# Who makes four of fourteen lower parts of the token operand at a change of phase: VectorE or GpSimd

## The chip, the cores and the metric

The kernel runs on one core of one Trainium2 chip. The metric is device time in microseconds, the median of several executions. The profile and the trace are of one more execution, taken by the hardware profiler, with times from the start of its span.

## What is computed

One inference step of a one-layer hybrid decoder: 1024 prompt tokens and 8 x 4 sample tokens (1056 in all), model width 2048, in float32. The two large products are the ones that matter here:

```
hn   = rmsnorm(x, g_norm)                    # 1056 x 2048
proj = hn @ w_in                             # 2048 -> 5904 columns, cut into groups A to D
...                                          # A: gated convolution, B: gated linear attention,
                                             # C: sliding-window attention, D: attention to memory
mix  = concat(y_a, y_b, y_c, y_d)            # 1056 x 2048
y    = x + mix @ w_out                       # 2048 -> 2048
```

The states and caches of the groups are outputs too.

## The kernel before

**Layout.** The 1056 tokens lie along the free dimension, in two halves of 528 (`H`), and 128 features or columns on the partitions. A float32 operand is written as the sum of two rounded parts: an upper part made by a cast on ScalarE, and a lower part, the operand less its upper part, made by VectorE. A product is then three matmuls: upper by upper, lower weights by upper tokens, upper weights by lower tokens (L668).

**Seven products.** Column tiles are taken in pairs, and a pair's product over a 2 x 2 arrangement (two halves of the features by two column tiles, two halves of the tokens) is made with seven products in place of eight, in the order B11, T2, B21, T1, T3, B22, T4. Each of the seven needs one combination of the token operand, called a strand, and one of the weights. A strand of one phase covers 4 feature tiles of 128, that is 128 x 2112 values, and stays in SBUF as an upper and a lower tile (`self.S[i]`, from the pool `sp` with 14 buffers) for all pairs of the phase. The weights' combinations are made anew for each product (`make_weights`, cast at L644, lower part at L645, sums at L626 to L640), two products ahead.

**Four phases.** The features are worked off in two halves for `w_in` and two for `w_out`: phases one to four. `first_pair` makes a pair's seven products in the first half of a product's features and its result is written to DRAM (`keep`); `second_pair` loads it back as a base (L736, L745), ScalarE copies it into PSUM (L751), and the seven products are added onto it. Results leave PSUM through ScalarE copies (L701 to L718, L757, L764) and VectorE additions (L698, L761 to L778).

**The change of phase.** The strands of phase one are split by `first_strands`. For the three others they were written to DRAM by `combine` (`self.xs`), and the generator `strands` loads and splits them: 7 strands in two halves of 128 x 1056 each, 14 parts, at about 590, 1186 and 1383 us. It is advanced once after each product (`after`). From the last pair of the old phase on, it takes two new buffers for strand `i` (those which the old strand `i` gives back), and splits two halves: a cast at L429 on ScalarE and a subtraction at L430 on VectorE each. After each half the next load is issued (L563, queue SP) into a buffer of the pool `rt`, 10 buffers of 128 x 1056, which bases, results and other tiles use as well. So a load waits until the subtraction of an earlier part has given its buffer back. The first loads, `depth` of them (3, 2 and 6 at the three changes), are issued ahead. The parts are counted from 0 here: part `2*i + j` is half `j` of strand `i`.

**Order.** Each engine works off its own queue in order. The source gives the order in which work is asked for; the layer under it decides, when the program is built, in which order each engine's queue gets it and puts the waits in. In the trace the first subtraction at L430 (593.7 us) stands ahead of an addition at L698 that the source asks for earlier. PSUM has two tiles for the projections (`pj`), so a product can't begin before an earlier one's result has been read out, and in `second_pair` not before its base has been copied in. GpSimd is used for masks, a few clearings and seven subtractions of 128 x 512 at the start (L366).

```
        for c in range(2):
            for kk in range(4):
                ...
                for n, (w, x) in enumerate(((wh, sh), (wl, sh), (wh, sl))):
                    nc.tensor.matmul(ps[:, 512 * c : 512 * c + CG], w[:, ks], x[:, xs],
```

Of the kernel before, what the change touches and what calls it, by code (L numbers as in the profile page):

```python
# [7 lines left out]
F32 = mybir.dt.float32  # L8
# [3 lines left out]
ALU = mybir.AluOpType  # L12
# [110 lines left out]
class _Step:  # L123
# [291 lines left out]
                nc.vector.tensor_tensor(dst[:, cs], ps[i][c][:, 0:CW], self.R[:, cs], op=ALU.mult)  # L415


    def split(self, i, src, half=None):


        nc = self.nc
        if half is None:
            self.S[i] = self.stile(), self.stile()
        h, l = self.S[i]
        src = src if isinstance(src, list) else [src]
        w = 4 * H // len(src) if half is None else 2 * H
        for n, x in enumerate(src):
            s = slice((half or n) * w, (half or n) * w + w)
            nc.scalar.copy(h[:, s], x)  # L429
            nc.vector.tensor_tensor(l[:, s], x, h[:, s].bitcast(F32), op=ALU.subtract)  # L430

    def first_strands(self):

# [121 lines left out]
    def strands(self, ph, depth):  # L555

        parts = []

        def load():
            i, j = divmod(len(parts), 2)  # L560
            if i < 7:
                t = self.rtile("sx")
                self.nc.sync.dma_start(  # L563
                    out=t.rearrange("p (k t) -> p k t", k=2),
                    in_=self.xs[ph][2 * j : 2 * j + 2, :, PLACE[i], :].rearrange("k p t -> p k t"))
                parts.append(t)
        for _ in range(depth):
            load()
        while not self.turn:
            yield  # L570
        for i in range(7):
            yield
            self.S[i] = self.stile(), self.stile()
            for j in range(2):
                self.split(i, parts[2 * i + j], j)
                load()
        yield

# [1361 lines left out]
```

## Time and profile before

| | us |
|---|---|
| median of 3 runs | 1571.45 (1569.26 to 1574.41) |
| the profiled execution | 1575.27 |
| its span in the trace | 1573.5 |
| TensorE busy, matmuls | 1530.4 (97%) |
| VectorE busy | 1105.2 (70%) |
| ScalarE busy | 772.6 (49%) |
| GpSimd busy | 23.3 (1%) |
| mean granted TensorE clock | 0.985 |
| subtractions at L430 in the three changes (42) | 51.6 |

In the trace PE is TensorE, PEld its weight loads, DVE VectorE, ACT ScalarE, POOL GpSimd, and SP the queue that issues the transfers. A row of the timeline gives the start, the duration, the engine, the line, the operation, output and inputs with their shapes, a count, and in brackets how long the engine sat idle ahead of it and what released it. In a row of stretches each engine has its busy time and number of instructions, then come the granted clock (1.00 is full), the share of the DMA engines and the rate in GB/s. A row of waits gives the total, the number and the longest.

### The profile page before, as it was taken

The numbers are of one execution on the slowest core, as the hardware profiler recorded it, in microseconds if no ns is written. First come the engines' busy times: TensorE is split into PE (matmuls) and PEld (weight loads), VectorE is DVE, ScalarE is ACT, GpSimd is POOL, SyncE is SP. The second block draws the span as 40 slices with busy tenths as digits, with TensorE's granted clock in tenths as the row PEclk, the third lists the DMA queues.
The fourth block names the chain that finished last, engine by engine and source line by source line (L and its number), as shares of the span: only waits on it lengthen the run. The fifth ranks groups of instructions, "written<-read, shape, count | busy, mean of one in ns | idle before, by whom it ended". The sixth has DMA issues, their size and how long they took to land.

```text
span 1573.5 us, 30753 instructions
## 1 busy us (share of the span) xinstructions
PE 1530.4 (97%) x12194; PEld 1459.6 (93%) x12194; DVE 1105.2 (70%) x2283; ACT 772.6 (49%) x1620; POOL 23.3 (1%) x35
## 2 busy tenths in 40 slices
PE   7889999999999999999999999999998999999998
PEld 7668999999999999988998999999988999999998
DVE  8998645586555559665767776967779777596664
ACT  8466633322333336744468774645557443363332
POOL 3000000000000000000000000000000000000000
PEclk9899999999999999999999999999999999999999
DMA  7523222375332248158423333533437224587651
GB/s 272 193 92 109 69 103 94 142 267 193 109 110 100 95 148 308 62 144 298 139 78 84 109 90 121 173 123 90 167 119 244 82 104 168 188 288 267 209 203 63
DMA packets 102418, 236.77 MB, mean 150 GB/s; under 512 B 16516, under 2 KB 22532, under 8 KB 102276
## 3 DMA queue, kind: packets, MB, share of 16 engines
q1 hardware_dynamic: 102276, 234.82, 44.4%
q8 instruction: 96, 1.57, 0.4%
q14 instruction: 46, 0.38, 0.1%
HBM read 165.38 MB, written 69.41 MB: 149 GB/s over the span
## 4 chain that ended last, share of the span: by engine, by line
PE 75%; DVE 13%; ACT 5%; DMA 4%; issue 3%; SPq 0%; DVEq 0%; ACTq 0%
PE pj L668 64%; PE ms L902 2%; DVE wl L645 2%; DMA sx<-xs 1%; DVE s L430 1%; DVE xhl L311 1%; ACT wh L644 1%; ACT t L1280 1%; PE ms L1037 1%; DMA x<-in_xT 1%; ACT xhl L310 1%; DMA kc<-in_cache_mem_kT 1%; DVE t L1267 1%; PE ms L1313 1%; PE ms L1007 1%
## 5 line engine op out<-in xcount | busy, mean ns | idle before, releaser
L668 PE MATMUL pj<-s,wh 128*128 128x264 f32 x6720 | 1268.7, 288 | 7.6 <-ACT pj L751 5.5
L668 PEld LDWEIGHTS pj<-s,wh 128*128 128x128 f32 x6720 | 1055.5, 189 | 25.6 <-issue 12.7
L668 PE MATMUL pj<-s,wl 128*128 128x264 f32 x3360 | 960.3, 286 | 0.8 <-DVE wl L645 0.8
L668 PEld LDWEIGHTS pj<-s,wl 128*128 128x128 f32 x3360 | 636.7, 190 | 5.9 <-issue 4.1
L644 ACT CAST wh<-wr 128x512 fp32r<-128x512 f32 x300 | 186.3, 621 | 262.4 <-PE pj L668 248.3
L645 DVE TENSOR_TENSOR wl<-wr,wh 128x512 fp32r<-128x512 f32 x300 | 206.5, 688 | 119.8 <-ACT wh L644 119.4
L698 DVE TENSOR_TENSOR d<-d,pj 128x528 f32<-128x528 f32 x180 | 121.4, 701 | 102.1 <-PE pj L668 60.0
L644 ACT CAST wh<-ws 128x512 fp32r<-128x512 f32 x120 | 74.5, 621 | 93.9 <-PE pj L668 89.5
L645 DVE TENSOR_TENSOR wl<-ws,wh 128x512 fp32r<-128x512 f32 x120 | 82.5, 688 | 9.1 <-ACT wh L644 8.5
L751 ACT COPY pj<-d 128x528 f32<-128x528 f32 x120 | 72.5, 604 | 15.1 <-DVE u L761 5.5
L430 DVE TENSOR_TENSOR s<-sx,s 128x1056 fp32r<-128x1056 f32 x42 | 51.6, 1250 | 1.9 <-ACT s L429 1.9
L429 ACT CAST s<-sx 128x1056 fp32r<-128x1056 f32 x42 | 44.3, 1075 | 10.0 <-DMA sx<-xs 5.2
L772 DVE TENSOR_TENSOR d<-d,pj 128x528 f32<-128x528 f32 x30 | 21.1, 703 | 36.5 <-PE pj L668 36.5
L701 ACT COPY d<-pj 128x528 f32<-128x528 f32 x30 | 18.0, 599 | 55.1 <-PE pj L668 55.1
L707 ACT COPY d<-pj 128x528 f32<-128x528 f32 x30 | 18.0, 601 | 53.4 <-PE pj L668 53.4
L1280 ACT ACTIVATE t<-t,sm,sm 128x256 f32<-128x256 f32 (+1 forms) x64 | 37.1, 581 | 14.2 <-DVE sm L1272 14.2
L640 DVE TENSOR_TENSOR wr<-wr,ws 128x512 f32<-128x512 f32 x60 | 41.8, 697 | 1.0
L775 DVE TENSOR_TENSOR d<-u,pj 128x528 f32<-128x528 f32 x30 | 21.1, 703 | 30.1 <-PE pj L668 30.0
L626 DVE TENSOR_TENSOR ws<-wr,wr 128x512 f32<-128x512 f32 x60 | 41.3, 688 | 1.2
L636 DVE TENSOR_TENSOR wr<-wr,wr 128x512 f32<-128x512 f32 x60 | 41.3, 688 | 1.1
L627 DVE TENSOR_TENSOR ws<-ws,wr 128x512 f32<-128x512 f32 x60 | 41.3, 688 | 1.0
L778 DVE TENSOR_TENSOR d<-u,pj 128x528 f32<-128x528 f32 x30 | 21.1, 703 | 29.8 <-PE pj L668 29.6
(368 smaller groups left out, 1524.2 us busy)
## 6 DMA issues: line engine op xcount, KB each, us to landing
wr<-in_w_in SPq DMA_DIRECT2D x184, 256.0 KB
half_in<-d SPq DMA_DIRECT2D x44, 528.0 KB
d<-half_in SPq DMA_DIRECT2D x44, 528.0 KB
sx<-xs SPq DMA_DIRECT2D x42, 528.0 KB
wr<-in_w_out SPq DMA_DIRECT2D x64, 256.0 KB
x<-in_xT SPq DMA_DIRECT2D x24, 528.0 KB
xs<-t SPq DMA_DIRECT2D x36, 264.0 KB
half_out<-d SPq DMA_DIRECT2D x16, 528.0 KB
```

What stands on the lines that cost most here:

```text
L429: nc.scalar.copy(h[:, s], x)
L430: nc.vector.tensor_tensor(l[:, s], x, h[:, s].bitcast(F32), op=ALU.subtract)
L626: v.tensor_tensor(s1, r(1, 0), r(1, 1), op=ALU.add)
L627: v.tensor_tensor(s2, s1, r(0, 0), op=ALU.subtract)
L636: v.tensor_tensor(x, r(0, 0), x, op=ALU.subtract)
L640: v.tensor_tensor(x, x, self.wsum[n][1], op=ALU.subtract)
L644: nc.scalar.copy(wh, x)
L645: v.tensor_tensor(wl, x, wh.bitcast(F32), op=ALU.subtract)
L668: nc.tensor.matmul(ps[:, 512 * c : 512 * c + CG], w[:, ks], x[:, xs], start=(first and kk == 0 and n == 0), stop=(kk == 3 and n == 2), ski ...
L698: nc.vector.tensor_tensor(o, o, bank(ps), op=op)
L751: nc.scalar.copy(bank(ps), x)
L1280: nc.scalar.activation(ps[u][:, g, kts[0] : 2], ps[u][:, g, kts[0] : 2], AF.Exp, bias=mx[:, c : c + 1], scale=rq[:, 4 * m + c : 4 * m + c ...
```

## The change

`split` gets an argument for the engine of the subtraction. `strands` passes GpSimd for the second half (`j` is 1) of the strands with even `i` (0, 2, 4 and 6), that is for parts 1, 5, 9 and 13 of the fourteen, at each of the three changes. The other ten parts, all casts, all loads and `first_strands` stay as they were.

```diff
-    def split(self, i, src, half=None):
+    def split(self, i, src, half=None, eng=None):
...
             nc.scalar.copy(h[:, s], x)
-            nc.vector.tensor_tensor(l[:, s], x, h[:, s].bitcast(F32), op=ALU.subtract)
+            eng = eng or nc.vector
+            eng.tensor_tensor(l[:, s], x, h[:, s].bitcast(F32), op=ALU.subtract)
...
             for j in range(2):
-                self.split(i, parts[2 * i + j], j)
+
+                self.split(i, parts[2 * i + j], j, self.nc.gpsimd if j and i % 2 == 0 else None)
                 load()
```

## The prediction

> **What bounds the kernel now.** I read the page first. Its first part says what is full and its fifth which instructions the change touches.
>
> ```profile
> span 1573.5 us, 30753 instructions
> PE 1530.4 (97%) x12194; PEld 1459.6 (93%) x12194; DVE 1105.2 (70%) x2283; ACT 772.6 (49%) x1620; POOL 23.3 (1%) x35
> L645 DVE TENSOR_TENSOR wl<-wr,wh 128x512 fp32r<-128x512 f32 x300 | 206.5, 688 | 119.8 <-ACT wh L644 119.4
> L430 DVE TENSOR_TENSOR s<-sx,s 128x1056 fp32r<-128x1056 f32 x42 | 51.6, 1250 | 1.9 <-ACT s L429 1.9
> ```
>
> TensorE sets the end: 97% of the span, and with the rows below nearly all of the rest is in gaps that a few places make. GpSimd is almost unused, VectorE is at 70% on average. An average does not decide: the 42 subtractions at L430 lie in three short stretches, the changes of phase (14 each). So I looked at those next, each cut into the pair of products before the change and the pair after it (for the second change the stretch in which its 14 parts are made).
>
> ```profile
> core 0: us, PE busy (x) PEld busy (x) DVE busy (x) ACT busy (x) POOL busy (x), PEclk, DMA share, GB/s
> 589.70:611.30 21.60, 20.36 (x168) 20.14 (x166) 21.37 (x26) 17.98 (x24) 0.00 (x0) 1.00 0.94 331
> 611.30:631.50 20.20, 18.99 (x152) 18.70 (x153) 16.07 (x23) 9.23 (x15) 0.00 (x0) 1.00 0.75 260
> 1186.20:1220.50 34.30, 30.23 (x216) 28.32 (x215) 30.68 (x48) 23.59 (x37) 0.00 (x0) 0.90 0.71 230
> 1383.30:1403.10 19.80, 17.64 (x146) 17.43 (x145) 19.77 (x24) 17.25 (x23) 0.00 (x0) 1.00 0.99 333
> ```
>
> Here VectorE is the full engine (21.37 of 21.60, 19.77 of 19.80), the DMA engines are nearly as full (0.94 and 0.99 of their time), GpSimd does nothing, and TensorE loses a little. What it loses stands in its own timeline as idle time ahead of an instruction:
>
> ```profile
> 611.31 0.39 PE L668 MATMUL pj<-s,wh 128*128 128x264 f32 x1 [1.26 <-ACT pj L751]
> 621.69 0.39 PE L668 MATMUL pj<-s,wh 128*128 128x264 f32 x1 [1.20 <-ACT pj L751]
> 1202.74 0.36 PE L668 MATMUL pj<-s,wh 128*128 128x264 f32 x1 [1.04 <-DVE d L772]
> 1212.38 0.59 PE L668 MATMUL pj<-s,wl 128*128 128x264 f32 x1 [0.81 <-DVE wl L645]
> 1403.06 0.56 PE L668 MATMUL pj<-s,wh 128*128 128x264 f32 x1 [2.17 <-ACT pj L751]
> ```
>
> The chain that ended last shows what stands behind the last of these: a subtraction gives a buffer back, the base of the next pair is loaded into it, and TensorE waits for that load.
>
> ```profile
> 1395.34 1.18 DVE s L430
> 1396.54 5.77 DMA d<-half_out
> 1403.06 164.96 PE pj L668 x1344
> ```
>
> The gaps at 611 and 621 have a second cause besides VectorE. ScalarE copies a base into PSUM (L751) only behind an instruction that waits for TensorE itself (L644 at 610.14, L764 at 620.53), so a faster VectorE alone does not close them:
>
> ```profile
> 610.14 0.62 ACT L644 CAST wh<-wr 128x512 fp32r<-128x512 f32 x1 [0.18 <-PE pj L668]
> 610.66 0.60 ACT L751 COPY pj<-d 128x528 f32<-128x528 f32 x1
> 620.53 0.60 ACT L764 COPY d<-pj 128x528 f32<-128x528 f32 x1 [1.60 <-PE pj L668]
> 621.03 0.61 ACT L751 COPY pj<-d 128x528 f32<-128x528 f32 x1
> ```
>
> **The change part by part.** It moves 12 instructions (parts 1, 5, 9 and 13 of the 14 at each of three changes, counted from 0) from VectorE to GpSimd. No transfer, no cast and no buffer is added.
>
> *Removed from VectorE.* 1.25 us each; back to back they cost less, by the first row below 2.42 us for two, so 1.25 - (2.50 - 2.42) = 1.17 us of queue each, 4.7 us at each change.
>
> *Added to GpSimd, and what that takes from VectorE.* No GpSimd instruction of 128x1056 is in the trace. The nearest are the subtractions of 128x512 at the start of the kernel:
>
> ```profile
> 1395.26 2.42 DVE L430 TENSOR_TENSOR s<-sx,s 128x1056 fp32r<-128x1056 f32 x2
> 27.76 2.31 POOL L366 TENSOR_TENSOR wl<-wr,wh 128x512 fp32r<-128x512 f32 x1
> 30.04 1.75 POOL L366 TENSOR_TENSOR r<-wr,r 128x512 fp32r<-128x512 f32 x1
> 31.75 1.76 POOL L366 TENSOR_TENSOR wl<-wr,wh 128x512 fp32r<-128x512 f32 x1
> 28.84 5.91 DVE L311 SCALAR_TENSOR_TENSOR xhl<-xr,consts,xhl 128x528 fp32r<-128x528 f32 x4
> 35.84 1.43 DVE L311 SCALAR_TENSOR_TENSOR xhl<-xr,consts,xhl 128x528 fp32r<-128x528 f32 x2
> ```
>
> These rows decide the case. Alone, two VectorE instructions of L311 take 1.43 us, so four take 2.86. While three GpSimd instructions ran, four took 5.91, that is 3.05 us more, 1.0 us for each GpSimd instruction. And a GpSimd instruction lasted 1.75 us, which is 1.0 of its own and 0.7 of one L311. The two engines took turns; neither worked beside the other. In proportion to the elements a moved subtraction would hold VectorE up for 1.0 x 1056/512 = 2.1 us; by VectorE's own two sizes, 1250 ns (L430) to 688 (L645), for 1.0 x 1.82 = 1.8. I take 2.0. The ends: 0, if it meets only VectorE work that isn't held up, and 2.1. A VectorE operation with both inputs in SBUF (L311, L430, L645) is what I take to be held; one that reads PSUM (L698, L761) I take to run on, which the trace does not show. Those that touch the projection's PSUM tile are 4.04 of the 21.37 us of VectorE's work in the first stretch:
>
> ```profile
> core 0: us, PE busy (x) PEld busy (x) DVE busy (x) ACT busy (x), PEclk, DMA share, GB/s
> 589.70:611.30 21.60, 20.36 (x168) 20.14 (x166) 4.04 (x6) 2.99 (x5) 1.00 0.94 331
> ```
>
> That is 19%. So a moved instruction holds VectorE up for 2.0 x 0.81 = 1.62 us on average and spares it 1.17: net +0.45 us, between -1.17 (no hold-up) and +0.93 (2.1 in full; +0.83 with 2.0).
>
> The Trainium skill has this as a rule. "SBUF — State Buffer", section "Who interferes with whom", says that a VectorE instruction with two SBUF inputs and a GpSimd instruction that reads SBUF need the same read port, and that the second to start waits for the whole of the first. The trace agrees, with 5.91 us in place of 2.86. The Trainium skill's "GPSIMD Engine Reference", section 3.1, gives 4497 ns for 2048 elements; an estimate from it by proportion is 2.3 us for 1056, with which the net would be 2.3 x 0.81 - 1.17 = +0.7 each and the sum below +4.9 in place of +3.15.
>
> *Where that reaches TensorE.* First change: VectorE is never idle from 589.7 to 611.3, so all four count up to the copies L751 that wait for it: 4 x 0.45 = +1.8 us. Second change: VectorE has idle time that swallows parts 1 and 5 (1.92 us) and part 13 (1.63 us), and part 9 alone stays, +0.45. Third change: the load of the base waits for the subtraction of part 6, so parts 1 and 5 count, +0.9; parts 9 and 13 end in idle time (0.57 and 1.00 us).
>
> ```profile
> 1200.72 1.26 DVE L430 TENSOR_TENSOR s<-sx,s 128x1056 fp32r<-128x1056 f32 x1 [1.92 <-ACT s L429]
> 1220.05 0.70 DVE L698 TENSOR_TENSOR d<-d,pj 128x528 f32<-128x528 f32 x1 [1.63 <-PE pj L668]
> 1410.72 0.70 DVE L761 TENSOR_TENSOR u<-u,pj 128x528 f32<-128x528 f32 x1 [0.57 <-PE pj L668]
> 1414.27 0.71 DVE L1852 TENSOR_TENSOR d<-d,x 128x528 f32<-128x528 f32 x1 [1.00 <-ACT d L764]
> ```
>
> *Costed at nothing.* The later end of the moved part itself: product i of the next pair needs strand i some six products after it is split, and a product takes about 21.6 / 7 = 3.1 us, so some 18 us cover a GpSimd instruction of 2 to 3 us. The queue behind it: GpSimd has no other work in these stretches. The SP queue: its next loads wait for the buffer that the subtraction frees,
>
> ```profile
> SPq L563 <- DVE s L430: 7.4, 6, 2.5
> ```
>
> (7.4 us over six loads at the first change), and the moved parts free theirs up to 0.9 us later; but GpSimd can start at once behind the cast, where VectorE came to it late, and the DMA engines have no room for earlier loads. If that cover is gone, the loads of the bases are late next.
>
> Sum: 1.8 + 0.45 + 0.9 = +3.15 us. The profiled execution took 1575.27 us (span 1573.5), 3.8 above the median of the runs, 1571.45; the terms are differences, so I set them on the median: **1574.6 us**. About 0.3% (4.7 us) is what a measurement of this kernel can tell from no change.
>
> **The rivals.**
>
> *Slower: the hold-up counts in full and the clock falls at the first change.* If GpSimd gets its turn between two operations of VectorE with SBUF inputs each time, the net is +0.83: 3.3 us at the first change, 1.7 at the second (parts 9 and 13), 1.7 at the third. Then the gap of 1.26 us at 611 grows past the length at which TensorE's granted clock falls. The point lies between 1.26 us, which left it at 1.00 (the first two stretches above), and 2.17 us, behind which it was
>
> ```profile
> 1403.00:1405.00 2.00, 1.94 (x9) 1.94 (x10) 2.00 (x4) 2.00 (x5) 0.00 (x0) 0.53 1.03 370
> 1405.00:1410.00 5.00, 5.00 (x37) 5.00 (x37) 5.00 (x6) 2.67 (x4) 0.00 (x0) 0.85 1.01 400
> ```
>
> 0.47 x 2.0 + 0.15 x 5.0 = 1.7 us lost. Together 3.3 + 1.7 + 1.7 + 1.7 = +8.4: 1579.9 us. For it: the rows of L366 show the turns without a miss. Against it: the fifth of VectorE's work that reads PSUM, and idle time at the second change.
>
> *Faster: VectorE is relieved.* If little is held up, part 6 is subtracted earlier at the third change. Its cast bounds that,
>
> ```profile
> 1393.21 2.05 ACT L429 CAST s<-sx 128x1056 fp32r<-128x1056 f32 x2
> ```
>
> which ends at about 1394.2 against a start at 1395.3: 1.1 us sooner, the gap falls to about 1.1 us, and the clock may stay up, 1.1 + 1.7 = 2.8. The second change loses its gaps of 1.04 and 0.81 us, and the first that of 1.20, where the order of the queues, planned anew, allows it. In all -5.9: 1565.6 us. Against it: the rows of L366, and ScalarE's order at 610 and 620.
>
> *Nothing happens.* The DMA engines are at 0.94 to 0.99 in these stretches, and each gap has an order on ScalarE or a load as its last cause; then VectorE's work moves inside the stretch and the time stays: 1571.5 us. This counts with the forecast, since the two cannot be told apart by time.
>
> **How the numbers follow.** Forecast with the third rival (-2 to +4.6 us, its own range 1569.5 to 1576): 0.54. Slower rival: 0.28. Faster rival: 0.18, which the rows of L366 keep low. The forecast lies near the upper bound of no change, which is why slower has the larger chance of the two. The range reaches to both rivals, from the weaker half of the faster one to just past the slower one: 1566 to 1580.5. Within 0.3%: 0.54, slower 0.28, faster 0.18.
>
> **What would show it.** Right: twelve GpSimd instructions of 128x1056, 2 us or more each; VectorE instructions with SBUF inputs that last 2 us longer beside them (an L645 of 0.69 us shown as about 2.7); VectorE's busy time no smaller in these stretches; the gaps at 611 and 1403 longer by 1 to 2 us. Wrong: L645 at 0.69 us beside a running GpSimd instruction, a gap at 1403 near 1 us without a fall of the clock, or another order on ScalarE that puts L751 ahead of L644. A gap of 2 us or more at 611 or 621 with a clock of 0.5 behind it is the slower rival. What I can't read from this trace is the order that the planner gives the queues once twelve instructions are elsewhere; that alone could move the time by a gap of 1 to 2 us either way.

## The result, and the profile after

| | us |
|---|---|
| before, median of the runs beside it | 1570.39 (1569.26 to 1574.41) |
| after, median | 1585.25 (1585.11 to 1585.8) |
| ratio | 1.0091, 95% interval 1.0074 to 1.0108 |
| the profiled execution after | 1585.11, span 1583.3 |

The change makes the kernel 14.3 us slower (11.6 to 17.0). Runs that something else had disturbed are left out of all ratios here. From the page after, the busy times and the groups of the weights' subtractions on VectorE and of the moved ones on GpSimd:

```profile
PE 1532.3 (97%) x12194; PEld 1462.0 (92%) x12194; DVE 1112.7 (70%) x2271; ACT 773.2 (49%) x1620; POOL 56.4 (4%) x47
L647 DVE TENSOR_TENSOR wl<-wr,wh 128x512 fp32r<-128x512 f32 x300 | 215.5, 718 | 118.5 <-ACT wh L646 118.2
L431 POOL TENSOR_TENSOR s<-sx,s 128x1056 fp32r<-128x1056 f32 x12 | 33.2, 2769 | 894.3 <-ACT s L429 727.5
```

Lines are up to two further down than before (L645 is L647, L698 is L700, L751 is L753, L612 is L614, L736 is L738). Twelve instructions left VectorE, and its busy time rose from 1105.2 to 1112.7 us. They had made 51.6 x 12/42 = 14.7 us, so everything else on VectorE became 14.7 + 7.5 = 22.2 us longer: 1.85 us for each GpSimd instruction. It can be seen on single rows, here of the first change (VectorE first, then GpSimd):

```profile
594.47 2.52 DVE L629 TENSOR_TENSOR ws<-ws,wr 128x512 f32<-128x512 f32 x1
599.86 0.69 DVE L700 TENSOR_TENSOR d<-d,pj 128x528 f32<-128x528 f32 x1
600.47 2.45 DVE L647 TENSOR_TENSOR wl<-wr,wh 128x512 fp32r<-128x512 f32 x1
...
593.96 2.47 POOL L431 TENSOR_TENSOR s<-sx,s 128x1056 fp32r<-128x1056 f32 x1 [441.15 <-ACT s L429]
599.91 2.47 POOL L431 TENSOR_TENSOR s<-sx,s 128x1056 fp32r<-128x1056 f32 x1 [3.47 <-ACT s L429]
```

An instruction of 0.68 us lasts 2.5 us when it starts behind a GpSimd subtraction: it ends 0.55 us after it (596.99 against 596.44, 602.92 against 602.38). L700, which reads one input from PSUM, keeps its 0.69 us; a clearer row, in which it starts behind GpSimd, stands with e7_hold below. Where TensorE loses time, in its timeline:

```profile
600.60 0.39 PE L670 MATMUL pj<-s,wh 128*128 128x264 f32 x1 [0.97 <-DVE d L700]
614.62 0.59 PE L670 MATMUL pj<-s,wh 128*128 128x264 f32 x1 [5.00 <-ACT pj L753]
1399.73 0.36 PE L670 MATMUL pj<-s,wh 128*128 128x264 f32 x1 [4.50 <-DVE d L700]
1413.26 0.39 PE L670 MATMUL pj<-s,wh 128*128 128x264 f32 x1 [3.03 <-ACT pj L753]
```

and the clock behind the three long gaps, by stretches (the granted clock is third from the end):

```profile
614.60:622.00 7.40, 7.38 (x47) 7.38 (x48) 6.96 (x8) 4.05 (x6) 0.72 (x1) 0.75 1.04 402
1399.00:1405.00 6.00, 5.27 (x31) 5.30 (x32) 4.12 (x5) 0.68 (x1) 0.00 (x0) 0.72 0.56 161
1413.00:1419.00 6.00, 5.74 (x34) 5.74 (x35) 5.73 (x4) 1.68 (x4) 3.40 (x1) 0.72 1.03 409
```

At the first change the gaps are 0.97 + 5.00 in place of 1.26 + 1.20, and 0.25 x 7.4 = 1.9 us go to the clock: +5.4. At the third they are 4.50 + 3.03 in place of 2.17, and 3.4 us of clock in place of 1.7: +7.1. That is 12.5 us; what the second change does is seen further down. The execution of before that was profiled (1575.27 us) is one of the longer ones: in e4_two and e11_one_sp, which have the third change as before, the gap there is 1.36 and 1.49 us with the clock at 1.00. Against those the third change loses about 9.5 us by the same sum.

**First change: a load that waits for a held instruction.** The SP queue in its timeline, before and then after:

```profile
598.03 0.34 SPq L612 DMA_DIRECT2D wr<-in_w_in  x1
598.43 4.90 SPq L563 DMA_DIRECT2D sx<-xs  x4
604.13 0.33 SPq L736 DMA_DIRECT2D d<-half_in  x1
```

```profile
598.79 4.51 SPq L614 DMA_DIRECT2D wr<-in_w_in  x2
603.35 2.43 SPq L564 DMA_DIRECT2D sx<-xs  x4
605.88 0.57 SPq L738 DMA_DIRECT2D d<-half_in  x1
```

and what SP waits for there (570 to 630 us), after:

```profile
SPq L614 <- DVE wl L647: 29.9, 9, 8.4
```

Before, the same wait (L612 for L645) was 26.0 us in all, the longest 7.4. The planner has put a second load of weights ahead of four loads of token parts and of the base (L738). Its buffer comes free with the subtraction L647, which GpSimd holds until 602.9; all five loads stand behind it until 603.3. ScalarE after shows where this goes:

```profile
608.27 1.07 ACT L429 CAST s<-sx 128x1056 fp32r<-128x1056 f32 x1 [3.33 <-DMA sx<-xs]
...
613.97 0.59 ACT L753 COPY pj<-d 128x528 f32<-128x528 f32 x1
```

It waits 3.33 us for the first of the four token parts, and the copy of the next pair's base stands in its queue behind the four casts. TensorE waits 5.00 us for that copy.

**Third change, first gap: two held instructions between two additions that free PSUM.** VectorE, before and after, from one addition L698 (L700) to the next:

```profile
1386.37 0.70 DVE L698 TENSOR_TENSOR d<-d,pj 128x528 f32<-128x528 f32 x1
...
1388.76 2.42 DVE L430 TENSOR_TENSOR s<-sx,s 128x1056 fp32r<-128x1056 f32 x2
1391.10 0.70 DVE L698 TENSOR_TENSOR d<-d,pj 128x528 f32<-128x528 f32 x1
```

```profile
1389.44 0.70 DVE L700 TENSOR_TENSOR d<-d,pj 128x528 f32<-128x528 f32 x1
1390.06 2.57 DVE L629 TENSOR_TENSOR ws<-ws,wr 128x512 f32<-128x512 f32 x1
...
1394.33 4.64 DVE L431 TENSOR_TENSOR s<-sx,s 128x1056 fp32r<-128x1056 f32 x2
1398.89 0.69 DVE L700 TENSOR_TENSOR d<-d,pj 128x528 f32<-128x528 f32 x1
```

4.73 us from addition to addition before, 9.45 after: 1.9 us of hold-up on L629, 2.2 on the pair of subtractions, and 0.6 for L629, which stood later in the queue before. TensorE needs the second addition for its PSUM tile: that is the gap of 4.50. As many subtractions (three) stand between the two additions as before: the new order has put a later part in the place of the moved one, so nothing is spared here.

**Third change, second gap: another order on ScalarE.** ScalarE, before and after, at the copy of the base into PSUM:

```profile
1402.40 0.60 ACT L751 COPY pj<-d 128x528 f32<-128x528 f32 x1 [2.23 <-DMA d<-half_out]
```

```profile
1410.15 1.07 ACT L429 CAST s<-sx 128x1056 fp32r<-128x1056 f32 x1 [0.28 <-PE pj L670]
...
1412.62 1.13 ACT L753 COPY pj<-d 128x528 f32<-128x528 f32 x2
```

Before, the copy waits for its load alone. After, it stands behind a cast that waits for TensorE's last products of the old pair, and behind two more casts: about 3 us in which TensorE has nothing to do (the gap of 3.03). This gap is not made by the hold-up: it is there, with 3.04 us, in e10_memset_sp and e13_memset_one_three, where nothing is held.

### The profile page after: what moved, and what is told of

It is laid out like the page before. It is cut to its first block, busy times and chain, and to the rows that moved or that the text cites. A ratio compares the mean times of both kernels' runs of the same rounds, so it can differ in the third digit from the quotient of the medians.

```text
span 1583.3 us, 30768 instructions
## 1 busy us (share of the span) xinstructions
PE 1532.3 (97%) x12194; PEld 1462.0 (92%) x12194; DVE 1112.7 (70%) x2271; ACT 773.2 (49%) x1620; POOL 56.4 (4%) x47
## 5 line engine op out<-in xcount | busy, mean ns | idle before, releaser
L670 PE MATMUL pj<-s,wh 128*128 128x264 f32 x6720 | 1272.6, 288 | 16.5 <-ACT pj L753 10.9
L670 PEld LDWEIGHTS pj<-s,wh 128*128 128x128 f32 x6720 | 1058.8, 190 | 34.2 <-issue 15.9
L647 DVE TENSOR_TENSOR wl<-wr,wh 128x512 fp32r<-128x512 f32 x300 | 215.5, 718 | 118.5 <-ACT wh L646 118.2
L700 DVE TENSOR_TENSOR d<-d,pj 128x528 f32<-128x528 f32 x180 | 121.4, 701 | 100.9 <-PE pj L670 58.5
L647 DVE TENSOR_TENSOR wl<-ws,wh 128x512 fp32r<-128x512 f32 x120 | 86.5, 721 | 9.7 <-ACT wh L646 9.1
L753 ACT COPY pj<-d 128x528 f32<-128x528 f32 x120 | 72.4, 604 | 13.5 <-DVE u L763 6.1
L431 POOL TENSOR_TENSOR s<-sx,s 128x1056 fp32r<-128x1056 f32 x12 | 33.2, 2769 | 894.3 <-ACT s L429 727.5
L629 DVE TENSOR_TENSOR ws<-ws,wr 128x512 f32<-128x512 f32 x60 | 45.0, 751 | 1.0
L703 ACT COPY d<-pj 128x528 f32<-128x528 f32 x30 | 18.0, 601 | 55.3 <-PE pj L670 55.3
L431 DVE TENSOR_TENSOR s<-sx,s 128x1056 fp32r<-128x1056 f32 x30 | 40.7, 1365 | 5.6 <-ACT s L429 5.6
L709 ACT COPY d<-pj 128x528 f32<-128x528 f32 x30 | 18.0, 601 | 54.3 <-PE pj L670 54.1
L1282 ACT ACTIVATE t<-t,sm,sm 128x256 f32<-128x256 f32 (+1 forms) x64 | 37.1, 581 | 14.3 <-DVE sm L1274 14.3
L720 ACT COPY d<-pj 128x528 f32<-128x528 f32 x30 | 18.0, 600 | 50.1 <-PE pj L670 50.1
```

What stands on the lines that cost most here:

```text
L431: eng.tensor_tensor(l[:, s], x, h[:, s].bitcast(F32), op=ALU.subtract)
L629: v.tensor_tensor(s2, s1, r(0, 0), op=ALU.subtract)
L647: v.tensor_tensor(wl, x, wh.bitcast(F32), op=ALU.subtract)
L700: nc.vector.tensor_tensor(o, o, bank(ps), op=op)
L753: nc.scalar.copy(bank(ps), x)
L1282: nc.scalar.activation(ps[u][:, g, kts[0] : 2], ps[u][:, g, kts[0] : 2], AF.Exp, bias=mx[:, c : c + 1], scale=rq[:, 4 * m + c : 4 * m + c ...
```

## The experiments

Three theories: the new order of the queues makes the loss (the loads above); the hold-up (VectorE kept waiting by GpSimd) makes it; or it needs both. Differences in us are (ratio - 1) x 1571, with the 95% interval in brackets.

| run | GpSimd's 12 operations | SP order at changes 1 and 3 | ratio | us |
|---|---|---|---|---|
| after | subtract | new | 1.0091 | +14.3 (+11.6 to +17.0) |
| e1_sp_order | subtract | old | 1.0071 | +11.2 (+7.1 to +15.1) |
| e2_order_only | none | new | 1.0033 | +5.2 (+2.5 to +7.7) |
| e4_two | subtract, change 2 alone | old | 0.9997 | -0.5 (-3.3 to +2.2) |
| e5_one_three | subtract, changes 1 and 3 | new | 1.0081 | +12.7 (+9.6 to +15.9) |
| e9_three | subtract, change 3 alone | new at 3 | 1.0045 | +7.1 (+4.7 to +9.6) |
| e11_one_sp | subtract, change 1 alone | old | 1.0003 | +0.5 (-1.4 to +2.4) |
| e6_memset | fill with zeros | new | 0.9999 | -0.2 (-2.5 to +2.0) |
| e10_memset_sp | fill with zeros | old | 0.9966 | -5.3 (-7.2 to -3.6) |
| e12_memset_two | fill with zeros, change 2 alone | old | 0.9955 | -7.1 (-9.4 to -4.7) |
| e13_memset_one_three | fill with zeros, changes 1 and 3 | old | 0.9995 | -0.8 (-3.0 to +1.3) |
| e7_hold | 4 more, at change 3, unused | old | 1.0023 | +3.6 (+1.7 to +5.7) |
| e8_hold_half | the same, half as wide | old | 1.0017 | +2.7 (0 to +5.2) |

**e1_sp_order: the change with the SP order of before.** The weights' load is tied behind the base's load at changes one and three. (By the trace SP then has the order of before but for one load of weights, issued some 8 us sooner at the first change; e10, e11 and e13 have the same.)

```diff
+            with self.tc.issue_after(behind) if behind else nullcontext():   # behind: the base's load
-            self.nc.sync.dma_start(out=t, in_=src[i][:, 512 * q : 512 * q + 512])
+                self.nc.sync.dma_start(out=t, in_=src[i][:, 512 * q : 512 * q + 512])
```

> The changed kernel, with one addition: at the first and third change the SP queue issues the weight load that the changed kernel has ahead of four token loads and the base's load behind them again, as the kernel before has it. GpSimd still makes the four parts. Theory A (queue order: the 12 to 15 us come from that one load, which waits on SP for VectorE and keeps the token loads behind it): nearly all goes, 1568 to 1573 us. Theory B (hold-up: GpSimd keeps VectorE waiting 1.8 us for each part, whatever the queues): nothing goes, 1581 to 1586 us. Theory C (both are needed: the hold-up makes the subtraction late for which the load waits): most goes, 1571 to 1577 us, with SP's wait gone and the VectorE instructions beside GpSimd still about 2.4 us long.

1581.48 us. At the first change the gap of 5.00 shrinks, the third stays as it is:

```profile
611.15 0.39 PE L673 MATMUL pj<-s,wh 128*128 128x264 f32 x1 [1.92 <-ACT pj L761]
1394.21 0.56 PE L673 MATMUL pj<-s,wh 128*128 128x264 f32 x1 [4.50 <-DVE d L705]
1408.56 0.39 PE L673 MATMUL pj<-s,wh 128*128 128x264 f32 x1 [3.04 <-ACT pj L761]
```

By the gaps, then, the SP order matters at the first change and not at the third, and is not the whole loss. By time alone this run and after can't be told apart, for their intervals overlap.

**e2_order_only: the kernel before with the SP order of after.** All 14 subtractions stay on VectorE; the load of weights is asked for earlier and the token load behind it.

```diff
+            if self.turn and self.in_first:
+                self.load_weights(n + 2, ((0, 0),))
+                self.behind = self.last_load                  # the next token load is issued behind it
```

> The kernel before, all 14 parts on VectorE, but with the changed kernel's order on SP at the first and third change: one weight load goes ahead of four token loads and the base's load. Theory A (queue order alone): the whole loss at these two changes, +9 to +13 us, 1579 to 1583 us. Theory B (hold-up alone): no change, 1569 to 1573 us. Theory C (both are needed): the load finds its buffer free soon, +0 to +4 us, 1570 to 1574 us.

1576.83 us, with gaps of 3.15 us at 609.06 and 3.69 at 1404.92. The order costs 5.2 us without GpSimd, a third of the loss. It is not SP's alone: with it the planner moved a few instructions on VectorE and ScalarE, a base's copy at the third change among them.

**e4_two and e5_one_three: one place at a time.**

```diff
-                self.split(i, parts[2 * i + j], j, self.nc.gpsimd if j and i % 2 == 0 else None)
+                self.split(i, parts[2 * i + j], j, self.nc.gpsimd if ph == 2 and j and i % 2 == 0 else None)
```

(`ph != 2` in the other.)

> The changed kernel with GpSimd's parts at the second change alone; the first and third change as before. By the two traces the second change took 2.3 us less with GpSimd. If that gain belongs to the moved parts: 1566 to 1569.5 us, faster than before. If it is chance (where the clock falls): 1569.5 to 1572. If the hold-up costs there too (theory B): 1572 to 1575.

> The changed kernel with GpSimd's parts at the first and third change alone; the second as before. If the stretches add up, the loss is 5.0 + 7.1 us there: 1582 to 1586 us, and with the run of the second change alone the two differences sum to that of the whole change.

1570.77 and 1584.24 us. The loss comes with the first and third changes; the second costs nothing in sum. That is not a change without effect but a sum of two, as e12_memset_two shows.

**e6_memset: VectorE relieved, nothing held.** GpSimd fills the 12 lower parts with zeros behind the same cast and reads nothing, so these lower parts are left out of the result. The order on SP, VectorE, ScalarE and TensorE is that of after.

```diff
-            eng.tensor_tensor(l[:, s], x, h[:, s].bitcast(F32), op=ALU.subtract)
+            if eng is nc.gpsimd:
+                ins = eng.memset(l[:, s].bitcast(F32), 0.0).ins      # behind the cast
+            else:
+                eng.tensor_tensor(l[:, s], x, h[:, s].bitcast(F32), op=ALU.subtract)
```

> The changed kernel with GpSimd's twelve subtractions replaced by clearings of the same 128x1056 that read nothing, each behind the same cast (so these lower parts are left at zero). SP, VectorE, ScalarE and TensorE have the same instructions in the same order as in the changed kernel. Hold-up theory (GpSimd keeps VectorE waiting while it reads SBUF, and this alone makes the gaps of 5.0, 4.5 and 3.0 us): the VectorE instructions beside GpSimd are back at 0.69 and 1.25 us, the gaps fall below 2 us each and the time to 1565 to 1574 us. Queue-order theory (the new order of the queues makes the gaps): they stay, 1579 to 1586 us. Both: in between, 1574 to 1579.

1570.31 us: with the same order and without the hold-up the loss is gone. In the timeline a VectorE instruction beside a fill, the fill, and the gaps that remain:

```profile
593.84 0.68 DVE L634 TENSOR_TENSOR ws<-ws,wr 128x512 f32<-128x512 f32 x1
593.30 0.98 POOL L432 MEMSET s<- 128x1056 f32 x1 [441.09 <-ACT s L429]
610.98 0.59 PE L675 MATMUL pj<-s,wh 128*128 128x264 f32 x1 [3.24 <-ACT pj L758]
1400.43 0.59 PE L675 MATMUL pj<-s,wh 128*128 128x264 f32 x1 [3.23 <-ACT pj L758]
```

The same subtraction of 128x512 that took 2.52 us beside a GpSimd subtraction takes 0.68 beside a fill. What the subtractions do and the fills don't is needed for the loss: 14.5 us lie between this run and after. That is the hold-up, and one thing more: a fill doesn't read the token part, so the part's buffer goes back for the next load without waiting for GpSimd. The gaps shown above at the first and third changes don't go back to such a wait; at the second change one does (e4_two, below). The Trainium skill states this difference in "SBUF — State Buffer", section "Who interferes with whom": a VectorE instruction with two SBUF inputs contends with a GpSimd instruction that reads SBUF, and not with one that only writes it. The trace agrees, 2.52 against 0.68 us. The first gap goes with the new SP order (e2_order_only had 3.15, and with the old order in e10_memset_sp it is 1.21); the one at the third change is that of ScalarE's order. Yet the time is that of before, so a gain must stand against them.

**e10_memset_sp: the same with the old SP order** (the edits of e1_sp_order and e6_memset together).

> GpSimd fills the 12 lower parts with zeros and reads nothing for it (so these lower parts are left out of the result), and the SP queue has the order of the kernel before at the first and third changes. VectorE is rid of 12 subtractions (14 us of its work), nothing holds it up, and no load is reordered. Theory that a relieved VectorE is worth nothing here because loads and ScalarE's order set the gaps: 1569 to 1572, as the kernel before, with the gap at 611 at 1 to 2 us and the one at 1400 at 2 to 3.3. Rival, that the new SP order had hidden a gain in the run with the zeros and the new order: 1565 to 1567, the gaps at 611 and 1400 near 1 us and no fall of the clock.

1565.08 us. My theory falls and the rival holds: relief of VectorE is worth 5.3 us once nothing is held and the loads keep their order. The new SP order costs the same 5 us here as in e2_order_only. In the two traces SP, VectorE, ScalarE and TensorE have one and the same order here and in e1_sp_order, so subtractions in place of fills cost 11.2 + 5.3 = 16.5 us. But the expected place was wrong too: the first gap is 1.21 us at 605.29, about as before, and 3.04 us stand at the third change (1393.32).

**e12_memset_two and e13_memset_one_three: where the gain is.** The fills at the second change alone, and at the two others alone (with the old SP order).

> Zeros in place of GpSimd's subtractions at the second change alone (four lower parts are left out of the result); the first and third changes are as before, and every queue has the order of the run with four subtractions at the second change alone, which took 0.9997 of the time before. Theory that relief and hold-up cancel there, and that the second change gives all the gain of the run with the zeros and the old SP order: 1565 to 1567, with the gaps of 0.6 to 1.0 us between 1202 and 1213 gone or under 0.6. Rival, that the gain lies in the first and third changes or is spread evenly: 1569 to 1571.

> The counterpart: zeros at the first and third changes (eight lower parts left out), the SP order of the kernel before there, and the second change as before. Theory that relief is worth nothing at these two, since a load and ScalarE's order end their gaps: 1570 to 1572. Rival, that relief is worth something at each change: 1566 to 1568.

1563.04 and 1569.98 us: all of the gain is at the second change. Stretches of 65 us around it follow for two kernels (behind the first comma stands TensorE's busy time; the clock as above). Before:

```profile
1185.00:1250.00 65.00, 60.40 (x457) 57.36 (x456) 57.34 (x139) 39.52 (x87) 0.00 (x0) 0.95 0.49 162
```

e12_memset_two:

```profile
1185.00:1250.00 65.00, 63.32 (x512) 61.15 (x511) 55.59 (x141) 42.48 (x97) 3.92 (x4) 1.00 0.51 170
```

Relieved and not held, TensorE is busy for 2.9 us more and the clock does not fall (0.05 x 65 = 3.3): 6.2 us, near the 7.1 measured. In other executions with this change as before the fall of the clock costs 1.7 us in place of 3.4 (e9_three, e11_one_sp), so the share of the clock is that of one execution. (The gain is relief together with the queue orders, TensorE's too, that the planner makes of it at this change; the two were not parted.) With real subtractions the same relief is used up: from e12_memset_two to e4_two, whose queues have one and the same order, the time rises by 0.42%, 6.6 us. Two gaps of e4_two show where it goes, each with the row that makes it (SP's waits are of 1180 to 1210 us):

```profile
SPq L564 <- POOL s L431: 6.5, 3, 2.8
1193.42 1.07 ACT L429 CAST s<-sx 128x1056 fp32r<-128x1056 f32 x1 [1.79 <-DMA sx<-xs]
1195.05 0.39 PE L670 MATMUL pj<-s,wh 128*128 128x264 f32 x1 [2.21 <-ACT pj L753]
...
1204.28 2.32 DVE L647 TENSOR_TENSOR wl<-ws,wh 128x512 fp32r<-128x512 f32 x1
1207.32 0.49 PE L1599 MATMUL ms<-qz,bw 128*128 128x128 f32 x2 [1.86 <-ACT bw L1535]
```

The second is the hold-up: the next instruction on VectorE, for which ScalarE's copy L1535 waits, comes behind L647. The first is a load that comes late: it waits until a GpSimd subtraction gives its buffer back (1189.2), the cast waits for the load, and a base's copy stands behind the cast. In e12_memset_two the casts before that copy have no such wait and the gap is 0.31. The 6.6 us are both together; no run parts them.

**e11_one_sp: the change at the first change of phase, old SP order.**

> The change at the first change of phase alone (4 subtractions on GpSimd), with the SP order of the kernel before. The first and third changes together lose about 13.5 us and the third alone 6.9, so the first with the new SP order is worth about 6.6 to 7.6. Theory that at the first change the loss needs both, the hold-up and the weight load that stands ahead of the token loads: 1571 to 1573, first copy out of PSUM after the change 1 to 2 us later than before. Rival, that the hold-up alone makes it: 1576 to 1578.

1572.18 us, 1.0003 (0.9991 to 1.0015). Four held instructions (the gap grows to 2.33 us at 613.98, against 1.26) cost no more than 2.4 us there, by the interval. With the new order the first change is worth 12.7 - 7.1 = 5.6, from e5_one_three and e9_three. The new order without GpSimd costs there, by the rows of e2_order_only, 3.15 us in place of 1.26 + 1.20 and 1.5 of clock: 2.2. So neither makes the loss of the first change by itself.

**e9_three: the change at the third change of phase alone** (`ph == 3`).

> The changed kernel with GpSimd's parts at the third change alone. If the third change carries most of the loss by itself, as the traces say (+7.1 us against a run of before that has a gap of 2.17 us there, more against one with a gap of 1.36): 1577 to 1581 us, and the first change the rest. If the two changes need each other, or the traces misplace the loss: 1571 to 1576.

1577.73 us, with gaps of 4.46 at 1392.42 and 3.03 at 1405.96: the loss of the third change stands by itself. The three changes one at a time with the old SP order at the first (e11_one_sp, e4_two, this run) sum to 0.5 - 0.5 + 7.1 = 7.1 us, where e1_sp_order has 11.2: its interval just reaches 7.1, so the sum is not confirmed.

**e7_hold and e8_hold_half: hold-up alone.** The kernel before, and beside it four unused GpSimd subtractions at the third change that read the cast tile (1056 or 528 columns). The order of all other queues is that of before, and VectorE keeps its 14.

```diff
+                if ph == 3 and j and i % 2 == 0:
+                    h = self.S[i][0][:, 2 * H : 2 * H + 1056].bitcast(F32)
+                    self.nc.gpsimd.tensor_tensor(self.scratch[:, 0:1056], h, h, op=ALU.subtract)
```

> The kernel before, all 14 parts on VectorE and every queue in its order, and beside it at the third change four GpSimd subtractions of 128x1056 whose result nobody uses, at the place where parts 1, 5, 9 and 13 have been cast. Hold-up theory: each holds VectorE up for 1.8 to 2.0 us, TensorE's gaps there grow by 4 to 8 us in all: 1574.5 to 1580 us. Queue-order theory: nothing, 1569 to 1572.5 us.

> As the run before with 128x528 in place of 128x1056, half the work of each of the four unused subtractions. Hold-up theory: about 1.0 us for each, half the loss, 1572 to 1576 us. Queue-order theory: nothing, 1569 to 1572.5 us.

1574.07 and 1573.11 us. Rows of e7_hold, VectorE and GpSimd:

```profile
1385.01 0.69 DVE L701 TENSOR_TENSOR d<-d,pj 128x528 f32<-128x528 f32 x1
1385.62 1.82 DVE L648 TENSOR_TENSOR wl<-wr,wh 128x512 fp32r<-128x512 f32 x1
1384.91 1.98 POOL L578 TENSOR_TENSOR scratch<-s 128x1056 f32<-128x1056 f32 x1 [3.88 <-ACT s L429]
```

Here GpSimd starts first and shows its own time, 1.98 us (1.95 in another turn); L701, which starts behind it and reads PSUM, keeps its 0.69, and L648 becomes 1.82. On the old order four such turns cost 3.6 us with nothing spared and no buffer given back later. The third change in the changed kernel costs 7.1; there the gap of 3.03 us that ScalarE's order makes comes on top. (The intervals of the two, +1.7 to +5.7 and +4.7 to +9.6, overlap, so the difference itself is not shown.) Half the width did not cost clearly less: the intervals of the two overlap for the most part, so this pair tells nothing on proportion.

## Why the prediction was wrong

It said 1574.6 (1566 to 1580.5, slower 0.28); it is 1585.25.

*Bound by TensorE, time lost in gaps at the changes of phase:* right. By the rows 12.5 us are lost in gaps at the first and third changes and to the clock behind them, where the runs have 14.3 us for the whole.

*Turns of the two engines:* right, also in size. 2.0 us x 0.81 = 1.62 was taken for a moved part, 1.85 came (nearly every turn met an instruction that is held); net of the relief +0.62 by the working above (1.85 less 14.7/12) in place of +0.45, inside the bounds. That an operation that reads PSUM runs on, assumed there, is shown by L701 at 0.69 us in e7_hold. GpSimd's own time, for which 2.3 us stood there as an estimate, is 1.95 and 1.98. The signs named for it came as said: L645 "about 2.7" is L647 at 2.45, and VectorE's busy time did not fall.

*Where that reaches TensorE:* here it failed. The step carried a mean net of +0.45 us per part from VectorE's queue to TensorE, as if what is spared and what is held met in one sum. They don't: a hold-up counts in full where the held instruction stands ahead of one that TensorE or SP waits for, and a spared 1.17 us counts only where VectorE is late. First change: +1.8 said; 5.4 by gaps and clock, 5.6 by runs. Third: +0.9 said, by way of the base's load; +7.1 by e9_three, and by way of the addition that frees PSUM and of ScalarE's order, which the step did not look at. (That the sum of the rows is 7.1 as well is luck in part, since it rests on a long execution of before.) Second: +0.45 said, with idle time of 1.92 and 1.63 us that swallows the rest; the runs show -7.1 with fills, and +6.6 for real subtractions in their place. The relief was mis-sized in part because the granted clock of 0.90 in that stretch was quoted and never priced: in the profiled executions half of the 6.2 us is clock.

*Costed at nothing, the SP queue:* failed. The cover named there, that the DMA engines had no room for earlier loads, did not matter; a load of weights moved ahead of the loads of token parts and of the base, and waited for a held instruction. "If that cover is gone, the loads of the bases are late next" is near what happened at the first change, where late token parts stood ahead of the base's copy on ScalarE. That GpSimd "can start at once behind the cast" did not hold at the second change: in e4_two a load waits up to 2.8 us for a GpSimd subtraction to give its buffer back, against "up to 0.9 us later". That the planner's order could move the time "by a gap of 1 to 2 us either way" was too little: 5.2 us by e2_order_only, 5 by e6_memset against e10_memset_sp.

*Slower rival, 1579.9:* the right mechanism at the first change (a gap beyond 2 us, the clock at half behind it), too low because it multiplied the same mean net by the number of parts. Its point between 1.26 and 2.17 us, at which a gap brings the clock down, does not exist as a length (last section). *Faster rival, 1565.6:* its sum is almost that of e10_memset_sp (1565.08), by chance, for its places are not: it gave 2.8 of 5.9 us to the third change, which gains nothing. It needs GpSimd not to hold VectorE up, as a fill does and a subtraction here does not.

What stays open: the new orders on VectorE and ScalarE were not tried by themselves, so the price of the gap of 3.03 us at the third change is known from rows alone; and at the second change hold-up and late buffers were not parted. No version that computes every lower part beat the kernel before.

## What to carry to other kernels

Work that was moved to GpSimd beside VectorE work with two SBUF inputs took back more than it spared here (22.2 us for 14.7). Price such a move by the instruction that stands behind each held one and by who waits for that, not by a mean over the queue. An edit that moves twelve instructions to another engine also has the planner write all queues anew, so compare the queue orders, SP first, before trusting a sum of durations. Where a stretch shows a granted clock below 1, a few closed gaps are worth that clock too: at the second change it made half of the gain in the profiled executions.

## What the runs showed of the hardware

The clock does not follow the length of a gap. In e10_memset_sp a gap of 3.04 us at the third change leaves it at 1.00, where 2.17 us had halved it in the profile before. The clock records of the traces show why. In each trace every fall to half starts on one grid of 3.41 us and lasts one, two or four of its steps (the last is cut off by the end of the trace). Before, falls start at 679.5, 962.8, 976.5, 1212.0 and 1403.1 us, which lie 83, 4, 69 and 56 steps apart. So the time can be cut along this grid. The step ahead of the fall at 1403.1 in before, and the two steps over which the gap of e10_memset_sp lies (behind the first comma stands TensorE's busy time):

```profile
1399.71:1403.12 3.41, 1.25 (x11) 1.04 (x9) 3.41 (x5) 1.19 (x3) 0.00 (x0) 1.00 0.96 315
```

```profile
1388.16:1391.57 3.41, 2.12 (x18) 1.92 (x16) 3.41 (x5) 3.12 (x5) 0.38 (x1) 1.00 1.05 402
1391.57:1394.98 3.41, 1.66 (x13) 1.66 (x14) 3.41 (x5) 2.23 (x4) 0.98 (x1) 1.00 1.02 409
```

A step with TensorE busy for 0.37 of it is followed by the fall; steps with 0.62 and 0.49 are not. At the three changes, in all fourteen traces, the steps ahead of a fall are busy for 0.54 or less, and those that no fall follows for 0.48 or more. So whether a gap of 2 to 3 us costs 1.7 us of clock besides depends on where it lies on the grid, which the kernel does not choose.

Not every fall is of this kind. In the profiled execution of e12_memset_two the clock stood near half for 14 us (four steps, from 1160.6) in which TensorE was never idle:

```profile
1160.00:1165.00 5.00, 5.00 (x31) 4.26 (x31) 3.12 (x10) 0.00 (x0) 0.00 (x0) 0.56 0.54 152
1165.00:1170.00 5.00, 5.00 (x27) 3.75 (x27) 3.65 (x7) 1.63 (x4) 0.00 (x0) 0.50 0.33 114
1170.00:1175.00 5.00, 5.00 (x22) 4.42 (x22) 3.97 (x8) 1.05 (x3) 0.00 (x0) 0.57 0.96 352
```

That execution took 1569.04 us, 6 more than the median of its kernel, which is about what such a stretch costs (0.44 + 0.50 + 0.43 of 5 us each, 6.9).

The Trainium skill, "TensorE: Matmul & The Clock Gate", part 1, has the clock fall after an idle window of about 3.4 us, and the window runs freely. The trace agrees on the window, with 3.41 us, and not on idle: a window that was busy for 0.37, in all traces up to 0.54, brought the fall. The fall without any gap in these rows that rule does not cover, and no run here shows its cause.

GpSimd does not always get its turn next. The last of the four subtractions in e7_hold took 5.47 us:

```profile
1403.29 5.47 POOL L578 TENSOR_TENSOR scratch<-s 128x1056 f32<-128x1056 f32 x1 [8.77 <-ACT s L429]
```

Behind its start four VectorE instructions with two SBUF inputs ran one after another at their own lengths (0.68 us, 2.41 for two, and 0.68, from 1403.33 on). It ended 1.88 us after the start of L764 (1406.88), which reads PSUM; by its own time of 1.95 to 1.98 us it got its turn only about there.
